# A two-block transformer step on one core: the convolution's second half follows its rows' request by 6.5 instead of 13 units of TensorE's work

## The chip, the cores and the metric

The kernel runs on one core of one Trainium2 chip. The metric is the time of one execution on the device in microseconds, the median of a few runs. The engines go by the profile's names: PE is TensorE (PEld its weight loads), DVE is VectorE, ACT is ScalarE, POOL is GpSimd, SP is SyncE, whose queue issues the transfers (DMA).

## The reference

Two blocks follow each other on 256 rows of 1024 values, in float32. The first block (two kinds of attention and a dense feed-forward) isn't touched. The second one, cut to what matters:

```python
h = rms_norm_2(x, norm1_g)
q, k, v, a, g = jnp.split(h @ w_in, splits, axis=-1)          # 512 columns each
attn = neighbourhood_attention(q, k, v, rpb)                  # 8 heads of 64
u = a * jax.nn.sigmoid(g)
dw = depthwise_conv(u, conv_w) + conv_b                       # 31 taps over the rows
conv = jax.nn.silu(layer_norm(dw, ln_g, ln_b))
mixed = concat([rms_norm_2(attn), rms_norm_2(conv)])
x = x + mixed @ w_out
x = x + expert_choice_ffn(rms_norm_2(x))                      # 16 experts, 32 rows each
```

The experts' three matrices are 1024x2048, 1024x2048 and 2048x1024, for each of 16 experts, and all of them are read from memory.

## The kernel before

A product in float32 is split in two parts: ScalarE copies the weights rounded into `wh`, VectorE makes the rest `wl` by subtraction (lines 288 and 289), and TensorE adds three products (`wh` and `wl` with the rows' high part `xt`, and `wh` with their low part). One *unit* is a quarter of a 512-column weight block for one half of the rows, six matmuls on 128x512. `linear_steps` (line 311) makes a block in eight units, four for each half of the rows (t = 0, 1), and hands each finished bank to an evacuation on ScalarE; what follows an evacuation on TensorE (transposes) is put off a while by `later`. The buffers of `wh` and `wl` are four each, so a unit of the next block is split when the same unit of this block has been used for both halves of the rows.

The second block has five flows, which `weave` (line 234) puts into one order. It counts TensorE's work in a clock of its own, some units of about a microsecond; a flow yields a number or the names of marks, and it goes on when so much work has been put out by the others or when the marks are set. The flows are:

- `block` (line 1132): the blocks of the input projection a and g (the gated input u of the convolution), q, k, v, and then the half of the output projection that belongs to the convolution (`mixc`).
- `conv` (line 1007): u is written to memory and read back as shifted rows `u4` by eight requests for each half of the channels (n = 0, 1). After the requests it yields 13.0, then TensorE multiplies 64 small products into two banks `sc`, and ScalarE adds the bias into `acc` (line 1023).
- `swish` (line 1046): for both halves of the rows, transposes of `acc`, layer norm on VectorE (lines 1055 to 1062), tanh on ScalarE (1064), the gate on VectorE (1065), the sum of squares on ScalarE (1067) and, later, transposes of the result `z` that give `mixc` (1038).
- `scores` (line 1078) and `values` (line 1097): the attention; the exponentials are on ScalarE (1093), the products of scores need all of q and k.

For q and k the evacuation is a copy `qk` (line 986), which TensorE transposes (line 255, `tr<-fst,qk`) and ScalarE puts into `qT` or `kT` (line 992).

TensorE's order is exactly that of `weave`. The orders of ScalarE and VectorE are made by the scheduler of the framework when the kernel is built; it puts each instruction where it expects it to become ready, and on the chip each engine then keeps to its own list. SyncE's list holds all transfers of weights, in the order of the program; each waits until its tile is free.

After the output projection come the router and the 16 experts (lines 1306 and 1330), with weights that stream through the tiles `slot` and `half`.

Of the kernel before, what the change touches and what calls it, by code (L numbers as in the profile page):

```python
# [145 lines left out]
def _program(nc, tc, A, dbg=None):  # L146
# [52 lines left out]
    def bank(tag, name=None):  # L199
        return psum.tile([128, 512], FT, tag=tag, name=name or tag, bufs={"mm": 2, "tr": 2, "sc": 3, "acc": 1}[tag])  # L200
# [30 lines left out]
    def mark(name, after=0.0):  # L231
        marks[name] = clock[0] + after
# [16 lines left out]
    def MM(out, lhsT, rhs, start, stop):  # L249
        T.matmul(out, lhsT=lhsT, rhs=rhs, start=start, stop=stop)  # L250
        n, m = math.prod(rhs.shape[1:]), math.prod(lhsT.shape[1:])
        clock[0] += max(n, 128) * (1 if rhs.dtype == FR else 4) / 2400 * min(m, 128) / 128
# [754 lines left out]
    def conv():  # L1007
        w = w_cv[0].rearrange("p (c j g m) -> p c j g m", c=4, j=4, g=8)
        for n in range(2):
            yield f"u{n}0", f"u{n}1"  # L1010
            u4 = [be2.tile([128, 4, 284], FT, tag="u4", name="u4", bufs=2) for c in range(2)]
            for c in range(2):
                for r in range(4):
                    nc.sync.dma_start(out=u4[c][32 * r:32 * r + 32], in_=udram[n][c, :, r:r + 284].rearrange("(j i) s -> i j s", i=32))
            yield 13.0
            for c in range(2):
                ps = bank("sc")
                for g in range(8):
                    for j in range(4):
                        MM(ps[32 * j:32 * j + 32, :256], w[:, 2 * n + c, j, g], u4[c][:, j, 4 * g:4 * g + 256], g == 0, g == 7)  # L1020
                    if g % 2:
                        yield 0
                S.activation(acc[:, 2 * n + c], ps[:, :256], AF.Identity, bias=cb[:, 2 * n + c:2 * n + c + 1])
        mark("conv", 0.81)
# [107 lines left out]
    def block():  # L1132
# [11 lines left out]
        flush()  # L1144

    weave(conv(), swish(), scores(), values(), block())
    a2.close()

# [134 lines left out]
    for e in range(NE):  # L1283
# [74 lines left out]
        with tc.manual_schedule(engines={mybir.EngineType.PE}):  # L1358
# [20 lines left out]
            for i in range(ng):  # L1379
# [5 lines left out]
                for at in range(0, 16 * w, min(step, 2048)):  # L1385
                    n = min(step, 2048)
# [44 lines left out]
```

## Time and profile before

| | |
|---|---|
| median of 3 runs | 1449.43 us (1449.01 to 1450.3) |
| the profiled execution, its own time | 1446.61 us |
| its span, first to last instruction | 1444.8 us |
| TensorE busy | 1118.9 us, 77% |
| VectorE busy | 419.9 us, 29% |
| ScalarE busy | 320.7 us, 22% |
| DMA | 498.15 MB, mean 345 GB/s |

The second block's flows lie at about 420 to 520 us, the router at 520 to 545 us, and the experts fill the rest, two thirds of the time. Shares over the whole span say little: up to the experts TensorE is busy nearly all the time and DMA is not, in the experts it is the other way round.

### The profile page before, as it was taken

How to read it: one execution, taken by the hardware profiler on the slowest of the kernel's cores; microseconds unless marked ns; L12 is line 12 of the kernel's file. 1: busy time of each engine (PE TensorE's matmuls, PEld its weight loads, DVE VectorE, ACT ScalarE, POOL GpSimd, SP SyncE). 2: the span in 40 equal slices, each digit the busy share in tenths (PEclk: the TensorE clock that was granted, in tenths of full speed). 3: DMA queues.
4: the chain of work that ended last, by engine and by line, in shares of the span. 5: the costliest groups of instructions: out<-in, count | busy, mean ns of one | idle time of the engine just before them, and what ended most of it. 6: DMA issues, size and time to landing. Idle time of an engine off the chain costs nothing.

```text
span 1444.8 us, 15517 instructions
## 1 busy us (share of the span) xinstructions
PE 1118.9 (77%) x6451; PEld 562.5 (39%) x6451; DVE 419.9 (29%) x800; ACT 320.7 (22%) x581; POOL 94.7 (7%) x69
## 2 busy tenths in 40 slices
PE   7989999999999989766775665777666577676565
PEld 5867877888877773111211111121111121111112
DVE  6576676545563651101100100001000111011002
ACT  5455646545564630000000000000000000000001
POOL 4433200010000000000000000000000000000001
PEclk9999999999999999887778888777887888778789
DMA  7623255757456779999999999999999999999997
GB/s 301 258 105 117 88 204 233 281 202 293 173 201 198 272 305 388 427 429 431 428 430 427 431 430 426 430 430 431 429 425 430 430 429 431 426 429 430 429 429 306
DMA packets 52165, 498.15 MB, mean 345 GB/s; under 512 B 6016, under 2 KB 9088, under 8 KB 12160
## 3 DMA queue, kind: packets, MB, share of 16 engines
q1 hardware_dynamic: 52096, 497.18, 83.5%
q8 instruction: 50, 0.82, 0.2%
q14 instruction: 19, 0.16, 0.0%
HBM read 495.52 MB, written 1.64 MB: 344 GB/s over the span
## 4 chain that ended last, share of the span: by engine, by line
DMA 59%; PE 32%; DVE 5%; ACT 2%; issue 1%; POOL 0%; SPq 0%; POOLq 0%; ACTq 0%; DVEq 0%
DMA half<-in_e_d 20%; PE mm L250 19%; DMA half<-in_e_u 18%; DMA slot<-in_e_g 8%; DMA slot<-in_e_u 4%; DMA half<-in_e_g 4%; PE dn L250 4%; PE mm L1306 3%; DMA slot<-in_e_dl 2%; PE sc L250 2%; PE tr L255 2%; DVE wl L289 1%; DMA slot<-in_w_a 1%; DMA half<-in_e_dl 1%; ACT wh L288 1%
## 5 line engine op out<-in xcount | busy, mean ns | idle before, releaser
L1306 PE MATMUL mm<-slot,xg 128*32 128x512 f32 x1536 | 238.8, 753 | 142.1 <-DMA slot<-in_e_u 92.4
L250 PE MATMUL mm<-wh,xt 128*128 128x512 f32 (+1 forms) x896 | 292.0, 396 | 4.6 <-DVE ropeb L447 3.2
L250 PEld LDWEIGHTS mm<-wh,xt 128*128 128x128 f32 x896 | 168.9, 189 | 43.4 <-issue 8.9
L250 PE MATMUL mm<-wl,xt 128*128 128x512 f32 (+1 forms) x448 | 174.8, 390 | 1.4 <-DVE wl L289 1.4
L1330 PE MATMUL sc<-half,hT 128*32 128x512 f32 x720 | 125.0, 780 | 65.5 <-DMA half<-in_e_d 65.4
L1337 DVE TENSOR_TENSOR x<-acc,x 128x512 f32<-128x512 f32 x60 | 41.5, 692 | 454.7 <-PE acc L1335 454.7
L1306 PEld LDWEIGHTS mm<-slot,xg 128*32 128x32 f32 x1536 | 47.3, 124 | 314.1 <-issue 125.6
L288 ACT ACTIVATE wh<-slot 128x1024 fp32r<-128x1024 f32 (+1 forms) x104 | 106.7, 1041 | 60.5 <-PE mm L250 47.8
L289 DVE TENSOR_TENSOR wl<-slot,wh 128x1024 fp32r<-128x1024 f32 (+1 forms) x80 | 99.1, 1249 | 65.5 <-ACT wh L288 64.9
L1335 PE MATMUL acc<-eo,owT 128*128 128x512 f32 x120 | 81.3, 764 | 22.4 <-DVE x L1337 11.0
L1313 DVE TENSOR_TENSOR sil<-sil,mm 128x512 f32<-128x512 f32 x16 | 11.0, 688 | 293.0 <-PE mm L1306 293.0
L1306 PE MATMUL mm<-half,xg 128*32 128x512 f32 x512 | 74.4, 666 | 26.6 <-DMA half<-in_e_u 16.1
L250 PEld LDWEIGHTS mm<-wl,xt 128*128 128x128 f32 x448 | 85.0, 190 | 18.0 <-DVE wl L289 2.1
L1351 ACT ACTIVATE eo<-sc 128x512 f32<-128x512 f32 x15 | 9.0, 597 | 358.4 <-PE sc L1330 358.4
L1330 PEld LDWEIGHTS sc<-half,hT 128*32 128x32 f32 x720 | 17.5, 122 | 164.1 <-DMA half<-in_e_d 138.5
L352 DVE SCALAR_TENSOR_TENSOR wl<-slot,pr,wh 128x512 fp32r<-128x512 f32 x88 | 62.8, 766 | 45.4 <-ACT wh L351 45.4
L1326 ACT ACTIVATE owT<-tr 128x256 f32<-128x256 f32 x16 | 6.1, 383 | 299.9 <-PE tr L1324 299.9
L289 POOL TENSOR_TENSOR wl<-slot,wh 128x1024 fp32r<-128x1024 f32 (+1 forms) x24 | 57.0, 2375 | 217.2 <-ACT wh L288 205.5
L351 ACT ACTIVATE wh<-slot,pr 128x512 fp32r<-128x512 f32 x88 | 58.1, 714 | 46.3 <-PE mm L250 31.4
L1372 POOL TENSOR_TENSOR x<-x,fing 128x256 f32<-128x256 f32 (+1 forms) x8 | 5.2, 659 | 896.7 <-ACT sq L1370 896.7
L1335 PEld LDWEIGHTS acc<-eo,owT 128*128 128x128 f32 x120 | 21.4, 224 | 91.2 <-ACT eo L1351 31.7
L1312 ACT ACTIVATE sil<-mm 128x512 f32<-128x512 f32 x16 | 9.6, 597 | 189.1 <-PE mm L1306 189.1
(330 smaller groups left out, 1042.7 us busy)
## 6 DMA issues: line engine op xcount, KB each, us to landing
slot<-in_e_g SPq DMA_DIRECT2D x48, 2048.0 KB, 24.4
slot<-in_e_u SPq DMA_DIRECT2D x48, 2048.0 KB, 29.2
half<-in_e_d SPq DMA_DIRECT2D x90, 1024.0 KB, 24.4
half<-in_e_g SPq DMA_DIRECT2D x32, 1024.0 KB, 29.3
half<-in_e_u SPq DMA_DIRECT2D x32, 1024.0 KB, 31.6
slot<-in_e_d SPq DMA_DIRECT2D x15, 2048.0 KB, 29.2
slot<-in_w_gu SPq DMA_DIRECT2D x11, 2048.0 KB, 8.2
slot<-in_w_a SPq DMA_DIRECT2D x7, 2048.0 KB, 8.3
```

Source lines behind the costliest of these rows:

```text
L250: T.matmul(out, lhsT=lhsT, rhs=rhs, start=start, stop=stop)
L255: T.transpose(out, src, ident if idn is None else idn)
L288: S.activation(h, src, AF.Copy)
L289: (G if pool else V).tensor_tensor(l, src, h.bitcast(FT), op=OP.subtract)
L351: S.activation(h, ps, AF.Identity, scale=col)
L352: V.scalar_tensor_tensor(l, ps, col, h.bitcast(FT), op0=OP.mult, op1=OP.subtract)
L1306: T.matmul(ps[32 * j:32 * j + 32], lhsT=xg[:, k, s0:s0 + 32], rhs=slot[kk][:, j * 512:(j + 1) * 512], start=k == 0, stop=k == 7)
L1312: S.activation(sil, gu[0], AF.Silu)
L1313: V.tensor_tensor(sil, sil, gu[1], op=OP.mult)
L1330: T.matmul(ps[32 * j:32 * j + 32, :c.stop - c.start], lhsT=hT2[:, q * 128 + 32 * j:q * 128 + 32 * j + 32], rhs=slot[n][:, j * 512 + c.star ...
L1335: T.matmul(ps, lhsT=owT[:, t * 128:(t + 1) * 128], rhs=eo, start=True, stop=True)
L1337: V.tensor_tensor(x[:, t, k], ps, x[:, t, k], op=OP.add)
```

## The change

One number in `conv`: after the requests for the rows of the second half of the channels (n = 1) the flow yields 6.5 instead of 13.0. The first half stays as it is.

```diff
@@ -1012,7 +1012,7 @@
             for c in range(2):
                 for r in range(4):
                     nc.sync.dma_start(out=u4[c][32 * r:32 * r + 32], in_=udram[n][c, :, r:r + 284].rearrange("(j i) s -> i j s", i=32))
-            yield 13.0
+            yield (13.0, 6.5)[n]
             for c in range(2):
                 ps = bank("sc")
                 for g in range(8):
```

Since `weave` sets TensorE's order by this number, and the scheduler sets the others' by TensorE's, the instructions of three engines move. Buffer numbers differ between the two kernels; `mm_3894` is the bank of k for the first half of the rows in both, `mm_3919` before and `mm_4007` now that for the second half. SyncE's and GpSimd's lists keep their order.

TensorE, the convolution's second half. Before, it stands behind the seventh of k's eight units:

```order
L250 MATMUL mm_3919<-wh_3886,xt_3465 128x512
L250 MATMUL mm_3919<-wl_3887,xt_3465 128x512
L250 MATMUL mm_3919<-wh_3886,xt_3466 128x512
L250 MATMUL sc_3952<-u4_3840,slot_2597 32x256 x32
L250 MATMUL sc_3986<-u4_3841,slot_2597 32x256 x32
L250 MATMUL mm_3919<-wh_3890,xt_3465 128x512
```

And now:

```order
L250 MATMUL mm_3894<-wh_3882,xt_3415 128x512
L250 MATMUL mm_3894<-wl_3883,xt_3415 128x512
L250 MATMUL mm_3894<-wh_3882,xt_3416 128x512
L250 MATMUL sc_3913<-u4_3840,slot_2597 32x256 x32
L250 MATMUL sc_3947<-u4_3841,slot_2597 32x256 x32
L250 MATMUL mm_3894<-wh_3886,xt_3415 128x512
```

It has moved behind the second of k's units, and five of k's units that stood ahead of it stand behind it now.

ScalarE, from the last copy of q (`qT`) on; `wh_4050` and the following are v's high parts before, `wh_4070` and the following now, `th2` belongs to the swish. Before:

```order
L992 ACTIVATE qT_3561<-tr_3901 128x4x128
L288 ACTIVATE wh_4050<-slot_4048 128x1024
L986 ACTIVATE qk_3932<-mm_3894,smalls_3535 128x512
L288 ACTIVATE wh_4054<-slot_4048 128x1024
L992 ACTIVATE kT_3562<-tr_3940 128x4x128
L288 ACTIVATE wh_4058<-slot_4048 128x1024
L1023 ACTIVATE acc_3563<-sc_3952,pr2_105 128x256
```

And now:

```order
L992 ACTIVATE qT_3561<-tr_3901 128x4x128
L1023 ACTIVATE acc_3563<-sc_3913,pr2_105 128x256
L1023 ACTIVATE acc_3563<-sc_3947,pr2_105 128x256
L288 ACTIVATE wh_4070<-slot_4068 128x1024
L288 ACTIVATE wh_4074<-slot_4068 128x1024
L1064 ACTIVATE th2_4000<-z_3553 128x512
L1067 ACTIVATE th2_4000,smalls_3535<-z_3553 128x512
L1064 ACTIVATE th2_4027<-z_3554 128x512
L986 ACTIVATE qk_4040<-mm_3894,smalls_3535 128x512
```

The copy of k's first half, `qk<-mm_3894`, has moved from behind v's first high part to behind v's second one and the swish's three instructions.

VectorE at the same place, now (`z_3553` and `z_3554` are the first and the second half of the rows):

```order
L1062 TENSOR_TENSOR z_3553<-z_3553,ln_3552 128x512
L289 TENSOR_TENSOR wl_4075<-slot_4068,wh_4074 128x1024
L1059 TENSOR_SCALAR z_3554<-sc_4015,smalls_3535 128x512
L1065 SCALAR_TENSOR_TENSOR z_3553<-th2_4000,z_3553 128x512
L1061 TENSOR_TENSOR z_3554<-z_3554,ln_3552 128x512
L1062 TENSOR_TENSOR z_3554<-z_3554,ln_3552 128x512
```

Before, these steps on z stood behind all of v's low parts and among the instructions of the first scores; now they stand among v's low parts.

TensorE, the transposes of the third group of probabilities (`e4`) and the products with them (`acc`). Before:

```order
L255 MATMUL tr_4364<-fst_103,e4_4183 128x128 x4
L250 MATMUL mm_4338<-wh_4305,mixc_4167 128x512
L250 MATMUL mm_4338<-wl_4306,mixc_4167 128x512
L250 MATMUL mm_4338<-wh_4305,mixc_4167 128x512 x2
L250 MATMUL mm_4338<-wl_4306,mixc_4167 128x512
L250 MATMUL mm_4338<-wh_4305,mixc_4167 128x512
L250 MATMUL acc_4355<-v2_3555,pt_4356 128x64
```

And now:

```order
L255 MATMUL tr_4353<-fst_103,on_4332 128x128 x4
L255 MATMUL tr_4365<-fst_103,e4_4189 128x128 x4
L255 MATMUL tr_4371<-fst_103,e4_4189 128x128 x4
L250 MATMUL acc_4362<-v2_3555,pt_4363 128x64
L250 MATMUL acc_4362<-v2_3555,pt_4364 128x64
```

The last unit of the convolution's half of the output projection (`mixc`) has moved from between them to ahead of them.

## Rows read from the trace of the kernel before

**Rows 1.** The page's part 4: shares of the chain, by engine.

```profile
DMA 59%; PE 32%; DVE 5%; ACT 2%; issue 1%; POOL 0%; SPq 0%; POOLq 0%; ACTq 0%; DVEq 0%
```

**Rows 2.** The chain in order of time: start us, us, engine and work.

```profile
568.91 3.48 PE sc L1330 x32
572.39 29.30 DMA slot<-in_e_g
...
1421.02 14.17 DMA half<-in_e_dl
```

**Rows 3.** Stretches: us, busy time of PE, PEld, DVE, ACT, POOL, granted clock, DMA share, GB/s.

```profile
548.00:549.00 1.00, 1.00 (x12) 0.25 (x8) 0.00 (x0) 0.00 (x0) 0.00 (x0) 0.50 0.00 0
...
551.00:552.00 1.00, 1.00 (x14) 0.32 (x16) 0.42 (x1) 0.00 (x0) 0.00 (x0) 1.00 0.85 336
```

**Rows 4.** Timeline of SyncE's queue: start us, us, line, transfer, count.

```profile
448.82 3.71 SPq L1014 DMA_DIRECT2D u<-udram  x8
...
477.62 0.33 SPq L216 DMA_DIRECT2D slot<-in_w_o  x1
...
549.23 1.23 SPq L806 DMA_DIRECT2D half<-in_e_g  x2
```

**Rows 5.** Timeline of TensorE around k and the convolution's second half (`u`).

```profile
458.25 0.63 PE L250 MATMUL mm<-wh,xt 128*128 128x512 f32 x2
...
465.87 7.11 PE L250 MATMUL sc<-u,slot 128*32 128x256 f32 x128
...
474.44 0.60 PE L255 MATMUL acc<-fst,acc 128*128 128x128 f32 x4
```

**Rows 6.** Timeline of TensorE: transposes of z, with idle time before and its releaser.

```profile
487.74 0.63 PE L255 MATMUL tr<-fst,z 128*128 128x128 f32 x4 [1.91 <-DVE z L1065]
```

**Rows 7.** Time to landing: of the eight requests `u`, and of one 2 MB load.

```profile
DMA to landing us min/median/max: 2.3/3.2/3.7
...
slot<-in_bias SPq DMA_DIRECT2D x1, 2048.0 KB, 8.0
```

**Rows 8.** Timeline of ScalarE: copy of k, a high part of v, a tanh.

```profile
474.70 0.69 ACT L986 ACTIVATE qk<-mm,smalls 128x512 f32<-128x512 f32 x1 [1.17 <-PE mm L250]
475.28 1.05 ACT L288 ACTIVATE wh<-slot 128x1024 fp32r<-128x1024 f32 x1
...
485.28 0.61 ACT L1064 ACTIVATE th<-z 128x512 f32<-128x512 f32 x1
```

**Rows 9.** Timeline of VectorE: a low part of v, the steps on z.

```profile
476.37 1.23 DVE L289 TENSOR_TENSOR wl<-slot,wh 128x1024 fp32r<-128x1024 f32 x1 [0.19 <-ACT wh L288]
...
481.31 0.81 DVE L1059 TENSOR_SCALAR z<-sc,smalls 128x512 f32<-128x512 f32 x1
...
482.38 0.69 DVE L1065 SCALAR_TENSOR_TENSOR z<-th,z 128x512 f32<-128x512 f32 x1
482.98 0.69 DVE L1061 TENSOR_TENSOR z<-z,ln 128x512 f32<-128x512 f32 x1
483.70 0.69 DVE L1062 TENSOR_TENSOR z<-z,ln 128x512 f32<-128x512 f32 x1
```

**Rows 10.** Stretches around two idle times of TensorE, columns as in rows 3.

```profile
23.20:26.30 3.10, 0.00 (x0) 0.00 (x0) 2.98 (x5) 2.08 (x4) 1.58 (x1) 1.00 0.86 370
26.90:30.30 3.40, 3.40 (x9) 2.64 (x8) 3.03 (x5) 0.00 (x0) 3.40 (x2) 0.50 0.01 2
30.40:34.70 4.30, 4.30 (x20) 3.50 (x19) 0.75 (x1) 0.67 (x1) 3.01 (x3) 1.00 0.73 236
...
487.80:491.20 3.40, 3.40 (x20) 2.55 (x21) 2.33 (x7) 3.40 (x10) 0.00 (x0) 1.00 0.75 323
```

**Rows 11.** Timelines: third group's transposes, the unit behind them, ScalarE's copy.

```profile
511.49 0.66 PE L255 MATMUL tr<-fst,e 128*128 128x128 f32 x4 [0.68 <-DVE gx L1038]
511.90 0.48 PE L250 MATMUL mm<-wh,mixc 128*128 128x512 f32 x1
...
512.24 0.60 ACT L583 ACTIVATE pt<-tr 128x512 f32<-128x512 f32 x1
```

## Prediction, made before the changed kernel ran

> **What bounds the kernel now.** I read the chain that ended last first. Its shares by engine [rows 1] are led by DMA, and in order of time [rows 2] the chain is TensorE's until 572.39 us and from there to the end a string of expert weights, each waiting for the one before. So the last 870 us run at the pace of the memory, and nothing in them depends on the convolution. What can move the end is the moment at which that stream begins. The table by stretches [rows 3] shows the DMA engines with a share of 0.00 at 548 to 549 us and 0.85 at 551 to 552 us: before the stream they stand idle. The request that ends the idling is the first one for an expert's half tile [rows 4], at 549.23 us, and it waits until TensorE has consumed the half tile that it replaces. TensorE therefore sets the start of the stream, and a microsecond that TensorE loses or gains between 458 and 549 us should come out at the end one for one.
>
> Then I read that stretch. TensorE is busy nearly throughout. The convolution's second half stands at 465.87 us and takes 7.1 us [rows 5]. The longest idle time of the stretch up to 500 us is 1.91 us ahead of the second transposes of z [rows 6], where the order puts a transposition before VectorE has finished z.
>
> **The change part by part.**
>
> *The move itself.* The same 64 products run, with the same tiles. They now follow K's second unit instead of its seventh, that is just after the matmul at 458.25 us [rows 5], at about 458.6 us, 7.3 us earlier. The cost of the move in TensorE's own work is zero: the products and the units change places.
>
> *Are the rows there?* The eight requests for them are out at 448.82 + 3.71 = 452.5 us [rows 4] and land at most 3.7 us later [rows 7], at 456.2 us. There are 2.4 us to spare, so I cost this at nothing. SyncE's queue keeps its order.
>
> *The old idle time.* z is now made while K is multiplied, long before its transposes. The 1.91 us [rows 6] go: −1.9 us.
>
> *What is late next.* Here the change bites. The engines between have fixed orders too. On ScalarE the copy of K's first half out of its bank, qk, stood ahead of the second half of the convolution; now it stands behind wh of V's second unit and behind both tanh of the swish. TensorE's transposes of that copy stand at their old place, right behind K's second unit for the second half of the rows, and everything after them queues behind them: the rest of K, all of V, the scores. When that K unit ends, this has to happen, one after the other, before the transposes can start:
>
> ScalarE's wh of V's second unit, which needs the buffer that this K unit frees: 1.05 us [rows 8]. VectorE's wl of it: 1.23 [rows 9]. VectorE's first step on z of the second half: 0.81. Its step on z of the first half (line 1065): 0.69. Lines 1061 and 1062 on z of the second half: 0.69 + 0.69 [rows 9]. ScalarE's tanh of it: 0.61, and at last qk: 0.69 [rows 8]. The sum is 6.46 us. Neighbours on VectorE overlap a little (482.38 to 482.98 is 0.60 for a 0.69), some −0.3 in all, and hand-overs between engines add some 0.04 each (wh ends at 476.33, wl starts at 476.37), with the end of the matmul itself +0.35. I take +6.5 us, with 6.2 and 7.0 as ends (one start of the tanh in the trace came about 0.35 later than its input). z of the first half is no bound: its last step comes out at about the moment at which wl can start. TensorE is idle for nearly all of it. In the trace such a copy follows at once: that of K's second half starts at 474.70 us, 0.3 us after TensorE has gone on to the next work at 474.44 us [rows 5, 8], and nobody waits for it.
>
> *The clock after it.* TensorE idle for 3.1 us early in the kernel (23.2 to 26.3 us) was followed by a stretch of 3.4 us at a granted clock of 0.50, the lower level of 1.2 GHz, in which 9 matmuls ran; afterwards 20 ran in 4.30 us at 1.00 [rows 10]. Nine take 1.9 us at that rate, so the stretch cost 1.5 us. The idle time of 1.91 us [rows 6] left it at 1.00 in the 3.4 us that followed [rows 10]. The new idle time is twice as long as the first of these, so I take +1.5 us; the ends are 0 (the lower clock falls into the idle time) and 3.0 (two such stretches).
>
> The Trainium skill (TensorE: Matmul & The Clock Gate, Part 1) says that the low clock is the default state and that activity releases it, so an idle TensorE falls back. By that rule the sum has a clock term, 7.4 us; by the row behind the 1.91 us alone it would have none, 5.9 us. The row of the 3.1 us idle time agrees with the rule.
>
> *The last part of the values.* Before, six matmuls of the output projection stood between the transposes of the third group of probabilities and the products with them, from 511.90 us, and hid ScalarE's copy, which ended at 512.24 + 0.60 = 512.84 us [rows 11]. In the new order the projection is finished by then and the products follow the transposes at once. Their cover is gone: 512.84 − 511.90 gives +0.9, with the hand-over +1.0 us. The lower end is 0.85, the transposes' own end at 512.15 plus the copy; the upper 1.5, if VectorE's copy of the other half is late.
>
> *Who else is queued behind.* V's last low part comes later with everything else, by some 6.5 to 9 us, and the request for w_o2 waits for it (it left at 477.62 us, when wl of 476.37 us had ended [rows 4, 9]). A load of that size landed after 8.0 us [rows 7]. ScalarE's split of it stands ahead of eight exponentials and of the copies of V out of their banks, so these may come just too late for the second pair of projection units. By the durations, they come 0 to 1 us late: I take +0.3. The early request of e_g, which waits for the convolution's last product, goes out 7 us sooner; nobody waits for that load.
>
> *Sum:* −1.9 + 6.5 + 1.5 + 1.0 + 0.3 = +7.4 us. The profiled execution took 1446.61 us with a span of 1444.8 us; it becomes 1454.0. The median of the three runs is 2.8 us above the profiled one, 1449.43, and I put the sum on it: **1456.8 us**.
>
> **The rivals.**
>
> *Not slower: ScalarE gets to qk in time.* This needs ScalarE to pass over an instruction that waits, or the order at run time to be another than the built one. Then the new idle time is nought, the old one is gone and the tail costs 1.0: −0.9 us, 1448.5 us. It decides if qk is made by the end of the K unit ahead of its transposes. For it speaks that qk's own input is complete one K unit before that, some 7 us before its turn. Against it speaks the old idle time [rows 6]: TensorE, with units of V ready behind, stood still for one transposition. The Trainium skill (PSUM — Partial Sum Buffer, Engine vs sequencer instructions) says that ScalarE's and VectorE's queues are strict FIFO; by that this rival is out, and no row of ScalarE here shows a case that settles it. Chance 0.05.
>
> *Hidden behind the memory.* If the DMA engines had transfers waiting until 549 us, a late TensorE would cost nothing and the time would stay at 1449.4. The share of 0.00 at 548 us [rows 3] speaks against it. Chance 0.03.
>
> *The stall without the clock.* 7.4 − 1.5 = 5.9 us, 1455.3. The row behind the 1.91 us speaks for it, the one behind the 3.1 us against. Chance 0.22.
>
> *A larger one.* Two stretches at the lower clock and values that come a full microsecond late: 7.4 + 1.5 + 0.7 and the tanh's 0.35, some 10 us, 1459.4. Chance 0.10.
>
> **How the numbers follow.** The forecast has 0.60. Timing can tell about 0.2% here, 2.9 us. Slower by more than that: 0.60 + 0.22 + 0.10 = 0.92. Within 0.2%: the first two rivals, 0.08, of which I give 0.01 to faster, since the first would have to gain three times its sum: 0.07 and 0.01. The low end is the smallest stall without the clock, 6.2 − 1.9 + 0.85 = 5.1 us, less 0.8 us of scatter (the three runs lie within 1.3 us): 1453.7. The high end is the larger case, 10, with the same scatter: 1460.2. The first two rivals stay outside.
>
> **What would show it.** A row of TensorE with transposes of qk, and ahead of it an idle time of 6 to 7 us that ends with ScalarE's line 986; no idle time ahead of the transposes of z; a granted clock of 0.50 for a few microseconds after; the request for the half tile at 549.23 us some 7 us later, and the same gap of idle DMA before it; the stream itself unchanged in length. I am wrong if the transposes of qk start within 2 us of the K unit, or if the stream starts later but ends where it ended.

## The result, and the profile after

The changed kernel takes 1457.18 us, the median of five runs (1453.62 to 1460.45); the kernel before, beside it, 1449.01 us (1447.99 to 1450.3). The ratio is 1.0053, its 95% interval 1.0036 to 1.0069: slower by 5 to 10 us, about 0.5%. Forecast were 1456.8 us. The profiled execution after is the shortest of the five, 1453.62 us with a span of 1451.8 us.

On TensorE (start us, us, line, operation, operands, count, and in brackets the idle time ahead and what ended it) the second half of the convolution and what answers to [rows 5, 6] now stand so:

```profile
457.81 7.12 PE L250 MATMUL sc<-u,slot 128*32 128x256 f32 x128
...
471.17 0.39 PE L250 MATMUL mm<-wh,xt 128*128 128x512 f32 x1
477.85 1.11 PE L255 MATMUL tr<-fst,qk 128*128 128x128 f32 x4 [6.30 <-ACT qk L986]
...
485.17 0.60 PE L255 MATMUL tr<-fst,qk 128*128 128x128 f32 x4
...
487.01 1.03 PE L255 MATMUL tr<-fst,z 128*128 128x128 f32 x8
```

The convolution stands 8 us earlier than in [rows 5], with nothing idle ahead of it. The transposes of z stand in one piece: the 1.91 us of [rows 6] are gone. Ahead of the transposes of K's first-half copy TensorE idles for 6.30 us, until ScalarE's line 986. This is what ScalarE did in that time:

```profile
471.59 1.06 ACT L288 ACTIVATE wh<-slot 128x1024 fp32r<-128x1024 f32 x1 [2.13 <-PE mm L250]
472.81 0.63 ACT L1064 ACTIVATE th<-z 128x512 f32<-128x512 f32 x1 [0.16 <-DVE z L1062]
475.27 0.63 ACT L1067 ACTIVATE th<-z 128x512 f32<-128x512 f32 x1 [1.83 <-DVE z L1065]
...
476.59 0.63 ACT L1064 ACTIVATE th<-z 128x512 f32<-128x512 f32 x1 [0.60 <-DVE z L1062]
477.13 0.67 ACT L986 ACTIVATE qk<-mm,smalls 128x512 f32<-128x512 f32 x1
```

And VectorE, from the low part of V to the last step on z ahead of the second tanh:

```profile
472.69 1.22 DVE L289 TENSOR_TENSOR wl<-slot,wh 128x1024 fp32r<-128x1024 f32 x1
473.83 0.80 DVE L1059 TENSOR_SCALAR z<-sc,smalls 128x512 f32<-128x512 f32 x1
474.55 0.68 DVE L1065 SCALAR_TENSOR_TENSOR z<-th,z 128x512 f32<-128x512 f32 x1
475.15 0.69 DVE L1061 TENSOR_TENSOR z<-z,ln 128x512 f32<-128x512 f32 x1
475.87 0.69 DVE L1062 TENSOR_TENSOR z<-z,ln 128x512 f32<-128x512 f32 x1
```

TensorE's last unit ahead of the wait ends at 471.17 + 0.39 = 471.56 us; it frees the buffer for V's high part, with which ScalarE goes on at 471.59. The bank that line 986 copies had been complete one unit of six matmuls earlier, at about 470.2 us. ScalarE copied it at 477.13, some 7 us later, after it had twice stood idle, 1.83 and 0.60 us, at the head of its list, waiting for z.

Behind the wait the clock is low: it falls to 0.50 in the last microsecond of the wait and is back at 1.00 from 484 us on. Stretches, with the columns of [rows 3] (the granted clock is the third figure from the right):

```profile
477.90:481.30 3.40, 3.40 (x10) 2.85 (x11) 0.43 (x3) 1.32 (x3) 0.54 (x1) 0.50 0.00 0
481.30:484.70 3.40, 3.40 (x11) 2.68 (x10) 1.23 (x1) 1.44 (x2) 0.00 (x0) 0.66 0.00 0
484.70:488.10 3.40, 3.40 (x23) 2.75 (x23) 1.68 (x2) 3.02 (x4) 0.00 (x0) 1.00 0.01 2
...
555.00:556.00 1.00, 1.00 (x12) 0.34 (x16) 0.42 (x1) 0.00 (x0) 0.00 (x0) 1.00 0.02 8
558.00:559.00 1.00, 1.00 (x12) 0.28 (x12) 0.40 (x1) 0.00 (x0) 0.00 (x0) 1.00 0.88 328
```

The last two are the end of the DMA's idle gap and the start of the stream, as in [rows 3] but 7 us later. The request between them, in SyncE's queue as in [rows 4]:

```profile
556.05 1.18 SPq L806 DMA_DIRECT2D half<-in_e_g  x2
```

And TensorE's timeline with scores, projection and values, as in [rows 11]:

```profile
495.99 1.14 PE L250 MATMUL sc<-kT,qT 64*128 64x256 f32 x8
...
499.99 1.59 PE L250 MATMUL sc<-kT,qT 64*128 64x256 f32 x8
...
504.13 0.93 PE L250 MATMUL mm<-wh,mixc 128*128 128x512 f32 x2
...
519.95 0.66 PE L255 MATMUL tr<-fst,e 128*128 128x128 f32 x4 [0.68 <-DVE gx L1038]
...
521.36 1.77 PE L250 MATMUL acc<-v,pt 128*128 128x64 f32 x14 [0.37 <-ACT pt L583]
...
527.32 0.66 PE L255 MATMUL tr<-fst,on 128*128 128x128 f32 x4 [0.78 <-DVE on L1114]
```

For every kernel of this study the next table cuts the span of its profiled execution at three rows: the first transposes of a copy `qk` (of q), the second transposes of `on` (the end of the values), the first request of a half `e_g` (549.23 in [rows 4], 556.05 after). The four parts add up to the span. The last column but one names the stretch at clock 0.50 that follows a wait of TensorE between 455 and 510 us.

| kernel | to first qk | to second on | to request | to the end | low clock behind the wait | median us |
|---|---|---|---|---|---|---|
| before | 450.68 | 68.77 | 29.78 | 895.57 | none | 1449.01 |
| changed | 449.91 | 77.41 | 28.73 | 895.75 | 477 to 484 | 1457.18 |
| changed, e5 | 453.68 | 77.38 | 31.44 | 895.80 | 480 to 488 | 1457.47 |
| e1 tanh after the copies | 451.71 | 69.28 | 31.44 | 895.97 | none | 1450.70 |
| e7 and the cover back | 451.53 | 69.01 | 31.42 | 895.84 | none | 1449.60 |
| e9 e1 with z's transposes later | 450.93 | 66.68 | 31.91 | 895.78 | none | 1447.19 |
| e3 tanh between the copies | 451.91 | 74.20 | 30.16 | 897.03 | 481 to 488 | 1455.21 |
| e4 convolution one unit later | 452.37 | 76.18 | 31.02 | 896.93 | 478 to 485 | 1458.26 |
| e2 wait filled | 452.87 | 75.31 | 30.18 | 895.74 | none | 1457.64 |
| e6 wait filled, again | 452.42 | 74.93 | 30.03 | 895.82 | none | 1457.91 |
| e11 wait filled, third trace | 450.94 | 78.05 | 31.53 | 896.78 | none | 1459.19 (one) |
| e10 wait half filled | 450.80 | 77.22 | 31.37 | 895.81 | 477 to 485 | 1458.10 |
| e8 before, z's transposes later | 453.50 | 71.96 | 28.21 | 897.63 | 500 to 505 | 1453.08 |
| e12 before, with 5.84 us of work | 452.37 | 75.99 | 32.38 | 896.86 | 496 to 500 | 1457.16 |

The last part is 895.6 to 897.6 us in all fourteen, however late it begins. The first part is the same program in all of them and yet runs from 449.9 to 453.7 us; the third runs from 28.2 to 32.4. Every trace also has stretches at 0.50 between 515 and 563 us, which the table doesn't show: added up, some 7 us before, 7 and 10 in the two traces of the changed kernel, 10 in e1, 7 in e2 and e6, 20 in e11 and 14 in e12.

### The profile page after: what moved, and what is told of

It is laid out like the page before. It is cut to its first block, busy times and chain, and to the rows that moved or that the text cites. A ratio compares the mean times of both kernels' runs of the same rounds, so it can differ in the third digit from the quotient of the medians.

```text
span 1451.8 us, 15518 instructions
## 1 busy us (share of the span) xinstructions
PE 1112.8 (77%) x6451; PEld 559.0 (39%) x6451; DVE 420.6 (29%) x800; ACT 321.0 (22%) x581; POOL 93.4 (6%) x69
## 4 chain that ended last, share of the span: by engine, by line
DMA 60%; PE 30%; DVE 5%; ACT 3%; issue 1%; POOL 0%; SPq 0%; POOLq 0%; ACTq 0%; DVEq 0%
PE mm L250 18%; DMA half<-in_e_d 17%; DMA slot<-in_e_g 13%; DMA half<-in_e_u 9%; DMA half<-in_e_g 8%; DMA slot<-in_e_u 6%; PE dn L250 4%; DMA slot<-in_e_dl 2%; DMA slot<-in_e_d 2%; PE sc L250 2%; DVE wl L289 2%; PE tr L255 1%; PE mm L1306 1%; DMA slot<-in_w_o 1%; DMA slot<-in_w_a 1%
## 5 line engine op out<-in xcount | busy, mean ns | idle before, releaser
L1306 PE MATMUL mm<-slot,xg 128*32 128x512 f32 x1536 | 234.9, 742 | 146.0 <-DMA slot<-in_e_u 96.8
L1330 PE MATMUL sc<-slot,hT 128*32 128x512 f32 x240 | 38.4, 770 | 25.6 <-DMA slot<-in_e_d 25.6
```

The lines of the kernel that those rows point to most:

```text
L1306: T.matmul(ps[32 * j:32 * j + 32], lhsT=xg[:, k, s0:s0 + 32], rhs=slot[kk][:, j * 512:(j + 1) * 512], start=k == 0, stop=k == 7)
L1330: T.matmul(ps[32 * j:32 * j + 32, :c.stop - c.start], lhsT=hT2[:, q * 128 + 32 * j:q * 128 + 32 * j + 32], rhs=slot[n][:, j * 512 + c.star ...
```

## The experiments

**Is it ScalarE's list? (e1)** The tanh and what follows them are asked for 4 us later; TensorE's list stays that of the changed kernel, row for row; VectorE's, which the scheduler makes, differs a little too.

```diff
             E.tensor_tensor(z, z, ln[:, 1], op=OP.add)
+            yield 0.58
+        yield 4.0
+        for t in range(2):
+            z = zs[t]
             th = bl.tile([128, 512], FT, tag="tmp", name="th2", bufs=2)
...
-            yield 0.58
-        yield 6.66
+        yield 2.66
```

> TensorE's order is word for word that of the changed kernel, the early convolution included. Only the second half of the swish flow (tanh, its product, the square) is asked for 4 us later, after which ScalarE has the copy qk of K's first half ahead of both tanh instead of behind them. Theory (TensorE waits for that copy, and the lower clock follows the wait): the idle time ahead of the transposes of qk falls from 6.3 us to under 1 us, no stretch at clock 0.50 stands behind it, and the transposes of z wait 1 to 2 us as they did in the kernel before: 1449 to 1451.5 us. Rival (the early place of the convolution costs by itself, whatever ScalarE does): the time stays at 1455 to 1458 us.

Measured: 1450.7 us (twelve runs, 1447.89 to 1457.4), ratio 1.0019 (1.0008 to 1.0031). TensorE's timeline of e1:

```profile
473.19 0.60 PE L255 MATMUL tr<-fst,qk 128*128 128x128 f32 x4
...
481.83 0.66 PE L255 MATMUL tr<-fst,z 128*128 128x128 f32 x4 [1.63 <-DVE prm L1072]
```

And ScalarE's copy of K's first half, ahead of the first tanh at 477.25 us:

```profile
472.09 0.69 ACT L986 ACTIVATE qk<-mm,smalls 128x512 f32<-128x512 f32 x1 [0.83 <-PE mm L250]
```

The copy now waits for TensorE's matmul only. No wait ahead of the transposes of qk, 1.63 us ahead of those of z, no low clock behind: as expected, and the rival is out. The kernel before, beside this run, took 1448.64 us, so e1 loses 2.1 us where the changed kernel loses 8.2: with the convolution early and the same order of TensorE, some 6 us are back. The convolution's place costs through the list of ScalarE.

**How much of z's chain must stand ahead? (e4, e3)** e4 puts 7.5 in the changed line, so that only the first tanh stands ahead of the copy; e3 is e1 with two other numbers (its diff, against e1, is below), so that both tanh stand between the copies of K's two halves.

```diff
-            yield (13.0, 6.5)[n]
+            yield (13.0, 7.5)[n]
```

> The number of the changed line is 7.5 instead of 6.5 us: the convolution's second half then stands one unit of K later, and ScalarE has the copy of K's first half behind the first tanh alone, with the second tanh behind it. Theory (the price is the part of z's chain that stands ahead of the copy): the idle time ahead of the transposes of qk is 2 to 4 us instead of 6.3, with or without a stretch at the lower clock: 1451 to 1455 us. Rival (any early place costs the same): 1456 to 1458 us.

Measured: 1458.26 us (five runs, 1456.59 to 1458.69), ratio 1.0064 (1.0052 to 1.0076). TensorE's timeline of e4:

```profile
479.85 1.11 PE L255 MATMUL tr<-fst,qk 128*128 128x128 f32 x4 [5.84 <-ACT qk L986]
```

ScalarE's, ahead of that row:

```profile
478.59 0.63 ACT L1064 ACTIVATE th<-z 128x512 f32<-128x512 f32 x1 [3.49 <-DVE z L1062]
479.12 0.67 ACT L986 ACTIVATE qk<-mm,smalls 128x512 f32<-128x512 f32 x1
```

And VectorE's, ahead of that tanh:

```profile
476.66 1.29 DVE L1061 TENSOR_TENSOR z<-z,ln 128x512 f32<-128x512 f32 x2
477.87 1.29 DVE L1062 TENSOR_TENSOR z<-z,ln 128x512 f32<-128x512 f32 x2
```

The wait hardly shrank, and the estimate of 2 to 4 us was wrong: here VectorE's list takes lines 1061 and 1062 for both halves of z side by side (x2), so the first tanh waits for nearly as much work as the second did. The rival had the number. What it does not have is the reason: the releaser is still ScalarE's copy, behind a tanh behind VectorE.

```diff
-        yield 4.0
+        yield 1.0
...
-        yield 2.66
+        yield 5.66
```

> As the run with the tanh after the copies, but the second half of the swish is asked for 1 us later only: on ScalarE both tanh then stand behind the copy of K's first half and ahead of that of its second half. Theory: neither the transposes of K's first-half copy nor those of z wait more than 0.5 us, so of the sum only the lost cover in the values (0.9 us) and late copies of V (0.5 us) are left against 1.9 us gained: 1448 to 1450 us. Rival (the convolution's place costs by itself): 1455 to 1458. Second rival (the wait only moves to the copy of K's second half): 1451 to 1453.

Measured: 1455.21 us (six runs, 1452.08 to 1456.52), ratio 1.0039 (1.0025 to 1.0053). TensorE's timeline of e3:

```profile
473.40 0.60 PE L255 MATMUL tr<-fst,qk 128*128 128x128 f32 x4
...
482.07 1.12 PE L255 MATMUL tr<-fst,qk 128*128 128x128 f32 x4 [3.94 <-ACT qk L986]
```

ScalarE's, ahead of the second row (line 1068 is the tanh there):

```profile
480.81 0.63 ACT L1068 ACTIVATE th<-z 128x512 f32<-128x512 f32 x1 [2.27 <-DVE z L1062]
481.35 0.67 ACT L986 ACTIVATE qk<-mm,smalls 128x512 f32<-128x512 f32 x1
```

The first copy is free and the second one stuck, as the second rival has it; it cost more than that rival's 1451 to 1453, since the clock fell behind this wait too (481 to 488 us). The wait stands wherever the copy stands behind a tanh.

**Is the lower clock a price of its own? (e2, e5, e6, e10, e11)** TensorE gets transposes of a constant to do while it waits.

```diff
                 pt = bank("tr")
+                if name == "k" and not t:
+                    for j in range(52):
+                        T.transpose(pt[:, :128], fst[:, :128], ident)
```

> The changed kernel, with 52 transposes of a constant put on TensorE ahead of the transposes of K's first-half copy, in the same bank, so that it works while it waits. ScalarE's and VectorE's orders are those of the changed kernel, so the copy comes as late as there. Theory (the lower clock is a price of its own, paid for the idle time): the copy is still awaited for some 6 us, of which the added transposes fill 5 to 6, but the granted clock behind it stays at 1.00; the time falls by 3 us, to 1453 to 1455 us, and the runs lie closer together than the 7 us of the changed kernel. Rival (the clock would have fallen anyway, or costs nothing here): 1456 to 1458 us with a spread as before.

Measured: 1457.64 us (five runs, 1455.66 to 1458.58), ratio 1.0058 (1.0046 to 1.007). TensorE's timeline of e2:

```profile
474.35 5.84 PE L992 MATMUL tr<-fst 128*128 128x128 f32 x52
480.82 0.66 PE L255 MATMUL tr<-fst,qk 128*128 128x128 f32 x4 [0.62 <-ACT qk L986]
...
485.45 0.60 PE L255 MATMUL tr<-fst,qk 128*128 128x128 f32 x4
```

And the stretch behind the wait, columns as in [rows 3]:

```profile
480.80:486.00 5.20, 5.18 (x27) 4.33 (x28) 1.72 (x4) 3.65 (x6) 0.54 (x1) 1.00 0.00 2
```

On the spot the theory holds: the clock stays at 1.00, and from the first transposes of qk to the second it is 4.63 us instead of the 7.32 of the changed kernel (477.85 to 485.17). So the stretch at 0.50 costs 2.7 us there. The total doesn't show it. So both were run once more, side by side:

> The changed kernel itself once more, beside the three that follow and on their chip. Both theories of the clock expect 1455 to 1459 us; what it gives is the base for the run with the wait filled, and a second profile that tells where stretches at clock 0.50 lie before 460 us, right behind the wait, and between 520 and 560 us, so which of them belong to the change (only the one behind the wait, I expect) and which come and go.

> The changed kernel with 52 transposes of a constant in the wait, once more, beside the changed kernel on the same chip. Its first profile showed the wait (5.84 us of transposes and 0.62 of idling), clock 1.00 behind it, and 1457.64 us all the same. Theory now (the lower clock behind the wait costs 3 us between the transposes of qk and those of z, and the scores give about 1 us of it back): 1.5 to 2.5 us below the changed kernel's median of this call. Rival (the total doesn't feel it, since a stretch avoided here is followed by others elsewhere): within 1 us of it.

Measured: 1457.47 us for the changed kernel (1455.82 to 1460.07), 1457.91 for the filled one (1454.98 to 1463.35). The local gain is there again (77.38 to 74.93 in the table), the total again is not lower. Together the eleven runs of the filled kernel have a mean of 1457.9 us, the ten of the changed one 1457.4. e5 also shows which stretches belong to the change: the one behind the wait is in both traces of it. Early in the kernel, where nothing was changed, the same stretch has three different clocks in three traces. The kernel before, columns as in [rows 3]:

```profile
26.00:34.00 8.00, 7.63 (x26) 6.14 (x27) 4.78 (x6) 0.67 (x1) 6.52 (x4) 0.79 0.33 99
```

The changed kernel:

```profile
26.00:34.00 8.00, 7.34 (x34) 5.74 (x36) 5.09 (x7) 0.76 (x2) 7.11 (x4) 1.00 0.36 110
```

The changed kernel in e5:

```profile
26.00:34.00 8.00, 6.89 (x18) 5.46 (x19) 5.51 (x8) 0.02 (x1) 5.71 (x3) 0.57 0.29 75
```

Then 26 transposes instead of 52, and one more execution with the 52:

```diff
-                    for j in range(52):
+                    for j in range(26):
```

> The changed kernel with 26 instead of 52 transposes of a constant in the wait: 2.9 us of work at the full clock, 5.8 at the half, so that even at the half clock they end before the copy comes and can prolong nothing. Two things are open after the filled runs (1457.6 and 1457.9 us beside 1457.2 and 1457.5, though their two traces show 2.1 to 2.5 us gained up to the transposes of on). If in most executions the 52 transposes run at the half clock in part and so prolong the wait, this one is at 1454.5 to 1456.5 us. If the clock falls behind an idle rest of 3.4 us as it does behind 6.3 us, or if what is gained there is lost again later, it stays at 1457 to 1458 us; the trace then shows which, by a stretch at 0.50 behind the wait or none.

> One more look at the kernel with 52 transposes in the wait, whose two traces so far are among its three shortest executions of eleven. Theory that the transposes run at the half clock in the longer executions: if this execution is a long one (1457 us or more), its trace shows a stretch at 0.50 within the 52 transposes or behind them. Rival (the long ones are long for stretches before 460 us or between 530 and 560 us, as in every kernel here): the 52 take 5.84 us and the wait ends as in the other two.

Measured: 1458.1 us with 26 (1455.79 to 1460.17), 1459.19 in the one execution with 52. TensorE's half-filled wait in e10:

```profile
472.29 3.00 PE L992 MATMUL tr<-fst 128*128 128x128 f32 x26
478.74 1.11 PE L255 MATMUL tr<-fst,qk 128*128 128x128 f32 x4 [3.46 <-ACT qk L986]
```

And the stretch behind it:

```profile
478.70:484.70 6.00, 5.96 (x17) 4.89 (x18) 1.69 (x4) 2.38 (x4) 0.54 (x1) 0.54 0.00 0
```

The idle rest of 3.46 us is followed by the same low stretch as 6.30 us, and the total is the changed kernel's. The execution with 52 was a long one; TensorE's timeline of e11:

```profile
472.43 5.84 PE L992 MATMUL tr<-fst 128*128 128x128 f32 x52
```

And a later stretch of it:

```profile
521.00:535.00 14.00, 13.09 (x50) 11.29 (x50) 4.86 (x11) 1.95 (x4) 0.55 (x1) 0.51 0.89 349
```

The transposes took 5.84 us as in the two shorter ones, and the clock stayed at 1.00 behind them: they did not run at the half clock in this long execution, and that theory falls as far as one execution can tell. Instead 14 us with a busy TensorE went by at 0.51, far behind the wait, from 521 us on, where the rival had named 530 to 560.

**The same microseconds as work, without a wait (e12).** The 52 transposes in the kernel before, by the same edit.

> The kernel before, the convolution at its old place, with 52 transposes of a constant (5.84 us in the three traces that have them) on TensorE ahead of the transposes of K's first-half copy, where nothing waits in that kernel: work in place of the wait, without any idling. Theory (what TensorE loses in this stretch, waiting or working, comes out at the end one for one): 5.8 us above the kernel before, 1454 to 1455.5 us, with spans from the first half tile's request to the end as before (895.6 to 897 us). If it comes to 1457 us or more, 5.8 us of work cost as much as the wait and its lower clock together, and the clock is paid for the lateness or the work itself rather than for the idle time, which would also explain why filling the wait gained nothing. If it comes to 1452 or less, part of the delay is hidden.

Measured: 1457.16 us (five runs, 1455.29 to 1459.35) against 1448.82, ratio 1.0055 (1.0041 to 1.0069): 8.3 us for 5.84 us of work (5.9 to 10.0 by the interval, so the 5.84 lie just outside). The first branch of the expectation fell and the second came. In its trace (the table) the part up to `on` is 7.2 us longer than before, 5.84 and a stretch at the low clock behind the old wait for z, which is still there with 1.97 us (before, the same wait of 1.91 us left the clock at 1.00); the rest lies in the router's part, where a stretch of e12 stands at 0.52:

```profile
547.00:561.00 14.00, 11.34 (x56) 7.53 (x58) 6.86 (x25) 3.81 (x5) 0.00 (x0) 0.52 0.69 291
```

So a delay of 6 us seems to be paid with some 2 us more whether TensorE waits or works in it. This trace is of the longest of e12's five executions, and one trace of each kernel doesn't tell why; this stays open.

**The lost cover (e7).** The projection's last unit is held back by 2 us of TensorE's work, in e1's kernel.

```diff
-            yield from linear_steps(w_o2[0][:, n * 2048:(n + 1) * 2048], mixC, add_scaled("c", n), ks=range(4), own=[])
+            steps_ = linear_steps(w_o2[0][:, n * 2048:(n + 1) * 2048], mixC, add_scaled("c", n), ks=range(4), own=[])
+            for i, s in enumerate(steps_):
+                yield 2.0 if n and i == 2 else s
```

> The kernel with the tanh after the copies (1450.7 us), with one thing added: the last unit of the output projection's first part is held back by 2 us of TensorE's work, so that six of its matmuls stand between the transposes of the third group of probabilities and the products with them, as in the kernel before; six fewer stand ahead of the transposes of on. Theory (the lost cover costs 0.9 us): 1449.5 to 1450.2 us, and in the trace no idle time ahead of the third group's products, with 0.8 to 0.9 us less from the transposes of qk of Q to the second transposes of on. Rival (the cover hid nothing, since what ends later is ahead anyway): 1450.7, the same length of that stretch.

Measured: 1449.6 us (twelve runs, 1445.71 to 1452.43), ratio 1.0003 (0.9991 to 1.0015), where e1 had 1.0008 to 1.0031. The number is as expected, the trace only in part. TensorE's timeline of e7:

```profile
511.84 0.65 PE L255 MATMUL tr<-fst,e 128*128 128x128 f32 x4 [0.35 <-DVE gx L1038]
...
513.73 1.89 PE L250 MATMUL acc<-v,pt 128*128 128x64 f32 x16
...
517.76 2.00 PE L250 MATMUL acc<-v,pt 128*128 128x64 f32 x16 [1.25 <-DVE pt L581]
```

The third group's products wait no longer, but the fourth's wait 1.25 us for VectorE's copy, where e1 had 0.35. The stretch is shorter by 0.27 us, not 0.9 (69.28 to 69.01). Since the two intervals overlap, the median's 1.1 us are not shown to be the cover's.

**A version that beats both? (e8, e9)** In the kernel before, the transposes of z are put off, to be rid of its 1.91 us (the number is 8.6, where the expectation writes 8.66):

```diff
-        yield 6.66
+        yield 8.6
```

> The kernel before with its convolution where it was, and only the transposes of z asked for 8.66 us after the swish instead of 6.66: they stand one unit of V and one group of scores later, when z of both halves is there, and the projection keeps units between the last two groups of probabilities and their products. Theory (an idle time of TensorE in this stretch comes out at the end one for one): 1.9 us for the wait for z and up to 0.8 for the second cover are gained, 1446 to 1447 us, below both kernels. Rival (z's transposes then make the projection late, which is needed before the values): 1448.5 to 1450 us.

Measured: 1453.08 us (twelve runs, 1448.57 to 1455.66), ratio 1.0026 (1.0016 to 1.0036), slower. TensorE's timeline of e8:

```profile
497.42 0.50 PE L250 MATMUL mm<-wh,mixc 128*128 128x512 f32 x1 [1.70 <-ACT mixc L345]
...
499.93 0.74 PE L250 MATMUL mm<-wh,mixc 128*128 128x512 f32 x2 [1.78 <-DVE mixc L346]
```

The rival was right, and dearer than it said: the projection waits twice, 3.48 us, for the split of what the transposes give, and the clock is low behind (500 to 505 us). z itself is late here: its last step ends at 489.75 + 0.68 = 490.43 us, just ahead of its transposes at 490.58, so a later place for these only moves the wait. e9 makes a like move in e1's kernel, where z is early (the diff is against e1).

```diff
-        yield 2.66
+        yield 5.66
```

> The convolution early as in the changed kernel, the tanh after the copies as in the first run (1450.7 us), and the transposes of z asked for 3 us later than there, one unit of V and one group of scores further on; the order then also keeps six matmuls of the projection between the third group's transposes and products. z is made some 6 us earlier here than in the kernel before, so, unlike in the run that moved z's transposes in the kernel before (1453.1 us), the projection should not have to wait for it. Theory: 1.63 us of waiting for z and part of the 0.9 us of cover come back: 1447.5 to 1449 us, at or a little below the kernel before (1449.2). Rival (the projection waits for z's split as it did there, 1.7 + 1.8 us): 1451 to 1454 us.

Measured: 1447.19 us (twelve runs, 1445.11 to 1451.41), ratio 0.9988 (0.9977 to 0.9999): 0.1 to 3.3 us below the kernel before and 10 below the changed one. The part up to `on` is 66.68 us, 2.1 less than before, the transposes of z wait for nothing on TensorE:

```profile
481.49 1.03 PE L255 MATMUL tr<-fst,z 128*128 128x128 f32 x8
```

So the early convolution seems to be worth some 1.5 us once ScalarE's and TensorE's lists follow it. It is the best of several versions tried, and the interval ends just below 1, so this gain is not beyond doubt.

## Why the prediction was right, and where it wasn't

*What bounds.* TensorE sets the start of the stream. From the request to the end it is 895.57 us before and 895.75 after, and the DMA's gap ahead of it stands as in [rows 3]. The rival that memory hides the delay is out. That what TensorE loses comes out one for one is less sure: 5.84 us of work cost 8.3 in e12.

*The move and the rows.* No idle time stands ahead of the convolution at 457.81 us: costed at nothing, it costs nothing.

*The old idle time.* Gone, −1.9: VectorE's last step on z ends at 477.35 + 0.68 = 478.03 us, 9 us ahead of the transposes at 487.01. e8, where z is late, only moved the wait.

*What is late next.* Forecast 6.5 us (6.2 to 7.0), measured 6.30, by the chain that was named, link by link: wh 471.59, wl 472.69, line 1059, 1065, 1061, 1062, the tanh 476.59, qk 477.13 us. e1, e3 and e4 show it as the cause: the wait is there where the copy stands behind a tanh, and gone where it doesn't. The rival in which ScalarE passes over a waiting instruction is out by the row at 475.27: ScalarE idles for 1.83 us while the bank for line 986 has been complete since 470.2 us. The Trainium skill (PSUM — Partial Sum Buffer, Engine vs sequencer instructions) says that ScalarE's queue is strict FIFO; the trace agrees, which no row of before could settle.

*The clock after it.* Mis-sized: forecast 1.5 us, measured 2.7 where it stands (7.32 against 4.63 us for the same work in e2), within the ends 0 and 3.0. The step that failed is the price taken from [rows 10]: one low stretch of 3.4 us, where the new one lasts from 477 to 484 us, 6 of them behind the wait. And that price is of one execution: the same code comes out at a mean clock of 0.79, 1.00 and 0.57 in three traces. That the low clock comes with the wait is shown by both traces of the changed kernel and by e3, e4 and e10. The Trainium skill (TensorE: Matmul & The Clock Gate, Part 1) has an idle TensorE fall back to the low clock, and these traces agree; the 14 us at 0.51 with TensorE busy in e11 are not explained by it. What isn't shown is that the total pays 2.7 us for that stretch: filling the wait gained nothing in eleven timed runs (mean 1457.9 us against 1457.4), and 5.84 us of work without a wait cost 8.3. The rival "stall without the clock", 1455.3 us, is thus refuted on the spot but not by a total.

*The last part of the values.* Forecast 1.0. In before the second transposes of `on` stand here:

```profile
519.45 0.66 PE L255 MATMUL tr<-fst,on 128*128 128x128 f32 x4 [0.78 <-DVE on L1114]
```

From the third group's transposes [rows 11] it is 519.45 − 511.49 = 7.96 us to there, and 527.32 − 519.95 = 7.37 after, with 513.37 − 511.90 = 1.47 us of matmuls fewer: +0.9. The size was right; e7 shows that giving the cover back returns only 0.3 of it, as VectorE's copy for the fourth group is late then.

*Who else is queued.* Forecast 0.3 (0 to 1), measured 0.8: the last scores take 1.59 us where their neighbours take 1.14, and a pair of projection matmuls 0.93 where the pairs around it take 0.62. The second is the one forecast: the request for w_o2 left at 487.23 us, 9.6 later than before, ScalarE then stood idle for 3.75 us until the load had landed, at 495.44, and this pair waited for its copy of V, as TensorE's waits from 499 to 506 us (waiting, waited for, us in total, times, longest) have it:

```profile
PEld mm L250 <- ACT v L998: 0.5, 1, 0.5
```

The first was not: TensorE's waits put it down to VectorE (lines 346 and 1091), not to ScalarE.

*The sum.* −1.9 + 6.3 + 2.7 + 0.9 + 0.8 = 8.8 us; the trace has 77.41 − 68.77 = 8.6 up to `on`. Of that the profiled pair shows 7.0 in the span, since the part before the change is 0.8 us shorter and the router's 1.05, which no step had and which other traces of the same kernel do not repeat (453.68 and 31.44 in e5). The medians differ by 8.2. The forecast of 7.4 lies 0.8 below, and the likeliest case is the one that came: the wait and its releaser were foreseen, to 0.2 us. That the total agrees so well is in part luck. Without the clock term, which no total shows, the other terms give 6.1 us, and 2 of the 8.2 have no named cause.

## What to carry to other kernels

Before you move work on one engine, look in the lists of the others for what is now queued ahead of an evacuation that the first engine will want: here a copy of 0.67 us came some 7 us late because it stood behind two tanh, and asking for the tanh later took the wait away, and some 6 of the 8.2 us with it, without touching TensorE's list. A gap that the trace shows can be there because its input is late, and moving the consumer then only moves the gap (e8); move the producer first, then the consumer (e9).

## What the hardware showed beside that

An idle rest of 3.46 us behind 3.00 us of work was followed by the low clock just as 6.30 us of idling were (0.54 over 478.7 to 484.7 us in e10). Filling a wait of 6.5 us with work kept the clock at 1.00 there and gained nothing in all, and 5.84 us of added work cost 8.3 us; in the traces of e11 and e12 some 14 us stand at 0.51 and 0.52 later on, once with TensorE busy for 13.09 of 14.00 us. The code ahead of the change took 449.9 to 453.7 us in fourteen traces. So single executions of this kernel can't price a clock term below some 3 us.
